# The first loads of a two-layer decoder trunk: a quarter of x in two tiles, two loads of `up` begun by ScalarE, two warm products fewer

## The chip, the cores and the metric

The kernel runs on one core of one Trainium2 chip. The metric is the device time of one execution in microseconds; 0.2% of it is about 2 us. The engines are called by the profile's names: PE (TensorE), with PEld for its weight loads, DVE (VectorE), ACT (ScalarE), POOL (GpSimd) and SP (SyncE). SPq and ACTq are the queues on which SP and ACT issue loads.

## What is computed

Two layers of a decoder trunk on 256 tokens of width 1024. Only the first lines of the first layer matter here:

```python
def rms_norm(x, g):
    xf = x.astype(jnp.float32)
    y = xf * lax.rsqrt(jnp.mean(xf * xf, axis=-1, keepdims=True) + RMS_EPS)
    return (y * g.astype(jnp.float32)).astype(x.dtype)

def swiglu(x, w_gate, w_up, w_down):
    return (jax.nn.silu(x @ w_gate) * (x @ w_up)) @ w_down

for l in range(DEPTH):
    h = h + 0.5 * swiglu(rms_norm(h, ffn1_norm[l]), ffn1_w_gate[l], ffn1_w_up[l], ffn1_w_down[l])
    h = h + hybrid_mixer(...)
    h = h + 0.5 * swiglu(rms_norm(h, ffn2_norm[l]), ffn2_w_gate[l], ffn2_w_up[l], ffn2_w_down[l])
```

The weights of the first feed-forward are 1024 x 2816 for `gate` and `up`, 2816 x 1024 for `down`, in float32.

## The kernel before

Every float32 weight is loaded into a `raw` tile and split into two parts of a shorter type, a high part `wh` (a rounding copy) and a low part `wl` (what is left, by a subtraction). The normalised input is split in the same way into `xhl`. A product is then three products of parts, summed in PSUM: high by high, high by low, low by high. In `ffn` the high weights meet both parts of x in one "wide" product of 512 columns, and the low weights meet the high part in a "narrow" one of 256. The division by the root mean square comes later, so the products can begin before the whole of x is there.

The class `Weights` keeps the loads in order. `issue` (line 78) gives out `raw` tiles, five at a time, and begins their loads with `load` (line 89), on SP's queue; `pump` and `take` run the splits. For the first feed-forward of the first layer the loads are put in order by hand (line 260 on): `by_hand` is 4, so `issue` gives tiles to the first four raws and begins nothing, and the lines behind it call `load` and `load_x` one by one. The first raw of `gate` and of `up` (256 columns, all eight tiles of 128 rows) is cut into three loads: row tiles 0 and 1, row tiles 2 and 3, row tiles 4 to 7. `load_x(mp)` (line 188) loads a quarter of x, 256 of its 1024 columns for all 256 tokens, also on SP's queue. ACT issues one load of its own, the gains of the first norm, and then runs an exponential on a tile of ones, ahead of which its function table is loaded.

So the order on SP's queue is: x 0, gate 0, up 0, x 1, gate 1, up 1, x 2, x 3, gate 2, up 2, and on with the second raws. Each line of this list but gate 2 and up 2 is 256 KB.

What TensorE does meanwhile is written out in `opening` (line 467) and ahead of it. `warm_up(WARM)` runs six products of a tile of ones with itself, whose result nobody reads (float32 operands: each is two passes in the profile). Then the gains are turned into columns (`turn_gains`, line 176), and `turn(0)` transposes the first quarter of x, tile by tile, 128 columns each, two token tiles to each. `warm_up(BRIDGE)` puts three more such products behind it. Then for `m` in 0 and 1: ACT writes the high parts of two tiles of x and VectorE the low parts (`parts`, lines 326 and 329); GpSimd copies the high part of a piece of gate, VectorE makes its low part, ACT copies the high part of a piece of up, GpSimd makes its low part (`split`, lines 477 and 478); TensorE runs gate's wide and narrow products, turns the next quarter of x, and runs up's. At last come the second halves (row tiles 4 to 7), copied by GpSimd (line 533) and ACT (line 117). The engines run their own streams in order, and the streams meet at semaphores.

Of the kernel before, what the change touches and what calls it, by code (L numbers as in the profile page):

```python
# [18 lines left out]
P = 128  # L19
# [15 lines left out]
HID_BUFS = 6  # L35
DOWN_LAG = 4
OUT_TAIL = 3
WARM = 6
BRIDGE = 3
B_TURN, A_ROPE, B_STEP, A_ROOT, A_TURN, SUMS_STEP = 18, 18, 20, 22, 26, 29  # L40


# [13 lines left out]
class Weights:  # L56
# [29 lines left out]
                    self.load(self.n_dma, i)  # L86
            self.n_dma += 1

    def load(self, raw, i):
        at, src = self.raws[raw][1][i]  # L90
        self.nc.sync.dma_start(self.raw_tiles[raw][at], src)  # L91

    def pump(self, count=1, low=None):

# [47 lines left out]
def kernel(ctx: ExitStack, tc: tile.TileContext, x, ffn1_norm, ffn1_w_gate, ffn1_w_up, ffn1_w_down,  # L142
                      mix_norm, w_in, forget_bias, a_q_norm, a_k_norm, b_q_norm, b_k_norm, c_q_norm, c_k_norm,
                      w_out, ffn2_norm, ffn2_w_gate, ffn2_w_up, ffn2_w_down, const, out):
    nc = tc.nc
# [7 lines left out]
    at = ctx.enter_context(tc.tile_pool(name="at", bufs=1))  # L153
# [19 lines left out]
    def load_gains(i, g, eng):  # L173
        eng.dma_start(rows[i], g.rearrange("l (k p) -> (l k) p", p=P))
# [10 lines left out]
    G.affine_select(out=ident, in_=ones, pattern=[[-1, P]], compare_op=ALU.is_equal, fill=0.0, base=0,  # L185
                    channel_multiplier=1)

    def load_x(mp):
        cols = slice(256 * mp, 256 * mp + 256)
        nc.sync.dma_start(trunk[:, :, cols], x[0].rearrange("(t p) d -> p t d", p=P)[:, :, cols])  # L190

    load_x(0)
    load_gains(0, ffn1_norm, nc.scalar)
    A.activation(tmp(P), ones, AF.Exp)

# [8 lines left out]
    W = Weights(tc, raw_pool, split_pool)  # L204
# [57 lines left out]
    W.issue()  # L262
    for m in range(2):
        if m:
            load_x(m)
        for i in range(2):
            W.load(i, m)
    for mp in range(2, 4):
        load_x(mp)
    for i in range(2):  # L270
        W.load(i, 2)
    for m in range(2):
# [107 lines left out]
    def ffn(norm, nxt, aside=None, first=False):  # L380
# [86 lines left out]
        def opening():  # L467
# [20 lines left out]
            def turn(mp):  # L488

                ps = []  # L490
                for m in (2 * mp, 2 * mp + 1):
                    ps.append(bank("acc")[:, :S])
                    for t in range(2):
                        T.transpose(ps[-1][:, t * P:(t + 1) * P], trunk[:, t, m * P:(m + 1) * P], ident)  # L494
                return ps
# [11 lines left out]
            xT = turn(0)  # L507
            warm_up(BRIDGE)
            for m in range(2):
# [673 lines left out]
    def warm_up(n, begin=False):  # L1183
        for i in range(n):
            mm(warm[:, :P], ones, ones, begin and i == 0, i == n - 1)

    warm_up(WARM, True)
    norm = Norm(0, 0)
# [40 lines left out]
```

## Time and profile before

| | us |
|---|---|
| three runs | 1038.13, 1038.09, 1037.77 (median 1038.09) |
| the profiled execution | 1038.33 |
| its span, from the first to the last instruction | 1036.6 |
| PE, busy | 1032.3 |
| DVE, busy | 808.9 |
| ACT, busy | 591.8 |
| POOL, busy | 148.2 |

The span is what the trace covers; 1.7 us of the execution lie around it. Matmuls are pipelined and their ends are modelled, so a PE that is busy throughout may still stand for a tenth of a microsecond here and there; starts are the safer reading. In a timeline a line is: start, length, engine, line of the kernel, operation, what it writes and reads, shape, count, and in brackets the idle time of the engine before it with what ended it. All loads move on the same 16 DMA engines: 181.61 MB in the whole run, at a mean of 175 GB/s.

### The profile page before, as it was taken

The page shows a single profiled execution, that of the slowest core. Times are in us where ns is not written, and L with a number is a line of the kernel's source. Part 1 is how long each engine was busy: PE and PEld are TensorE (multiplying, and loading weights), DVE is VectorE, ACT ScalarE, POOL GpSimd, SP SyncE. Part 2 cuts the span into 40 slices and gives each one's busy share as a digit, 9 for nine tenths or more (in the row PEclk, how much of TensorE's full clock was granted, in tenths as well). Part 3 has the DMA queues.
Part 4 walks back from the last instruction along what each step waited for, and adds up shares of the span by engine and source line. Part 5 has one row for each costly group of instructions (what it writes and reads, how often), then busy time and mean ns, then how long its engine had stood idle before and what let it go on. Part 6 is the DMA issues. An engine that isn't in the chain of part 4 may idle for free.

```text
span 1036.6 us, 15084 instructions
## 1 busy us (share of the span) xinstructions
PE 1032.3 (100%) x5641; PEld 898.8 (87%) x5641; DVE 808.9 (78%) x1537; ACT 591.8 (57%) x1045; POOL 148.2 (14%) x177
## 2 busy tenths in 40 slices
PE   9999999999999999999999999999999999999998
PEld 8888888898888888888888888888988988888887
DVE  6978778789876877777788777787898768777776
ACT  6655555666854655555465555557676546555552
POOL 2003000167800000000000110002766000000000
PEclk9999999999999999999999999999999999999999
DMA  9674656555431364645645564664555224554631
GB/s 320 222 244 157 214 185 198 182 190 174 154 131 42 123 230 144 236 163 206 200 163 195 180 219 150 241 185 174 163 194 172 83 67 159 182 199 167 232 134 40
DMA packets 130808, 181.61 MB, mean 175 GB/s; under 512 B 7040, under 2 KB 104624, under 8 KB 130736
## 3 DMA queue, kind: packets, MB, share of 16 engines
q1 hardware_dynamic: 130704, 180.66, 51.5%
q8 instruction: 44, 0.72, 0.3%
q14 instruction: 28, 0.23, 0.1%
q10 hardware_dynamic: 32, 0.01, 0.0%
HBM read 179.60 MB, written 1.05 MB: 174 GB/s over the span
## 4 chain that ended last, share of the span: by engine, by line
PE 99%; DMA 1%; SPq 0%; DVE 0%; issue 0%
PE ps_gu L302 66%; PE ps_acc L302 30%; PE ps_acc L337 1%; PE ps_gu L1038 1%; PE ps_gu L1137 1%; DMA trunk<-in_x_dram 1%; PE ps_acc L739 0%; PE ps_acc L1038 0%; PE ps_gu L1071 0%; PE ps_acc L494 0%; SPq L91 0%; PE ps_acc L363 0%; PE ps_acc L1071 0%; SPq L190 0%; DVE trunk L376 0%
## 5 line engine op out<-in xcount | busy, mean ns | idle before, releaser
L121 DVE TENSOR_TENSOR wl<-raw,wh 128x1024 fp32r<-128x1024 f32 (+2 forms) x342 | 416.9, 1225 | 24.9 <-ACT wh L117 24.9
L117 ACT CAST wh<-raw 128x1024 fp32r<-128x1024 f32 (+2 forms) x341 | 343.0, 1036 | 5.7 <-PE ps_gu L302 4.9
L302 PE MATMUL ps_gu<-xhl,wh 128*128 128x512 f32 x1408 | 330.4, 390 | 0.0
L302 PEld LDWEIGHTS ps_gu<-xhl,wh 128*128 128x128 f32 x1408 | 262.7, 188 | 53.9 <-ACT wh L117 0.4
L302 PEld LDWEIGHTS ps_gu<-xhl,wl 128*128 128x128 f32 x1408 | 176.1, 191 | 4.2 <-issue 0.2
L302 PE MATMUL ps_gu<-xhl,wl 128*128 128x256 f32 x1408 | 179.1, 283 | 0.0
L302 PE MATMUL ps_gu<-wh,xhl 128*128 128x512 f32 (+2 forms) x512 | 157.2, 377 | 0.0
L441 DVE TENSOR_TENSOR tmp<-ps_gu,tmp 128x256 f32<-128x256 f32 x176 | 72.9, 422 | 107.7 <-ACT tmp L440 107.4
L302 PE MATMUL ps_acc<-wh,hh 128*128 128x512 f32 (+1 forms) x352 | 137.2, 390 | 0.0
L302 PE MATMUL ps_acc<-wl,hh 128*128 128x512 f32 (+1 forms) x352 | 137.0, 389 | 0.0
L302 PE MATMUL ps_acc<-wh,hl 128*128 128x512 f32 (+1 forms) x352 | 136.5, 388 | 0.0
L440 ACT COPY tmp<-ps_gu 128x256 f32<-128x256 f32 x176 | 63.5, 371 | 93.3 <-PE ps_gu L302 93.1
L302 PEld LDWEIGHTS ps_gu<-wh,xhl 128*128 128x128 f32 x512 | 94.8, 188 | 14.6
L455 ACT CAST hh<-tmp 128x256 fp32r<-128x256 f32 x80 | 32.6, 407 | 120.0 <-DVE tmp L452 120.0
L302 PE MATMUL ps_gu<-wl,xhl 128*128 128x512 f32 (+2 forms) x256 | 95.7, 374 | 0.0
L447 ACT ACTIVATE tmp<-tmp 128x256 f32<-128x256 f32 x88 | 36.9, 419 | 81.9 <-DVE tmp L445 81.6
L313 POOL TENSOR_TENSOR y_n<-msq,minus_half 128x2 f32<-128x2 f32 x6 | 6.8, 1141 | 529.7 <-DVE msq L312 529.7
L302 PEld LDWEIGHTS ps_acc<-wh,hl 128*128 128x128 f32 x352 | 66.1, 188 | 13.9
L302 PEld LDWEIGHTS ps_acc<-wh,hh 128*128 128x128 f32 x352 | 66.2, 188 | 12.6
L302 PEld LDWEIGHTS ps_acc<-wl,hh 128*128 128x128 f32 x352 | 66.3, 188 | 12.2
L302 PEld LDWEIGHTS ps_gu<-wl,xhl 128*128 128x128 f32 x256 | 48.2, 188 | 6.7
L326 ACT ACTIVATE xhl<-ps_acc,gT 128x256 fp32r<-128x256 f32 x48 | 19.1, 474 | 39.2 <-PE ps_acc L337 35.7
(221 smaller groups left out, 1010.8 us busy)
## 6 DMA issues: line engine op xcount, KB each, us to landing
raw<-in_ffn_w_down_dram SPq DMA_DIRECT2D x44, 1024.0 KB, 4.9
raw<-in_ffn_w_gate_dram SPq DMA_DIRECT2D x42, 1024.0 KB, 6.6
raw<-in_ffn_w_up_dram SPq DMA_DIRECT2D x42, 1024.0 KB, 7.5
raw<-in_w_in_dram SPq DMA_DIRECT2D x24, 1024.0 KB, 4.9
raw<-in_w_out_dram SPq DMA_DIRECT2D x8, 1024.0 KB, 4.9
raw<-in_w_in_dram SPq DMA_DIRECT2D x4, 768.0 KB, 4.9
raw<-in_w_in_dram SPq DMA_DIRECT2D x4, 656.0 KB, 4.0
raw<-in_ffn_w_gate_dram SPq DMA_DIRECT2D x3, 512.0 KB, 7.1
```

The source lines that it names most:

```text
L117: self.nc.scalar.copy(hv, src)
L121: (engine or self.nc.vector).tensor_tensor(lv, self.srcs[self.n_low], hv.bitcast(F32), op=ALU.subtract)
L302: T.matmul(o, l, r, start=start, stop=stop, skip_group_check=True)
L313: G.tensor_tensor(y, dst, minus_half[:, :n], op=ALU.pow)
L326: A.activation(self.h[:, m], src, AF.Copy, scale=gT[:, self.col + m:self.col + m + 1])
L337: T.transpose(ps[:, i, t * P:(t + 1) * P], trunk[:, t, (2 * mp + i) * P:(2 * mp + i + 1) * P], ident)
L440: A.copy(o, ps[:, 1])
L441: V.tensor_tensor(o, ps[:, 0], o, op=ALU.add)
L447: A.activation(th, t_, AF.Tanh, scale=0.5)
L455: (V.tensor_copy if late else A.copy)(hh, t_)
L1038: T.transpose(b[:, j * P:(j + 1) * P], pj[i][:, j * P:(j + 1) * P], ident)
L1137: T.transpose(b[:66, i * S + t * P:i * S + (t + 1) * P], src[t][:, 2 * hp_ + i, :], ident)
```

## The change

`WARM` goes from 6 to 5 and `BRIDGE` from 3 to 2. `load_x` counts in tiles of 128 columns now; the first quarter of x is begun as two loads of one tile, the other three quarters as one load of two tiles each. `load` takes a queue, and `up`'s first two loads are begun by ACT, behind its exponential in its stream, in place of SP. The order on SP's queue becomes: x tile 0, x tile 1, gate 0, x 1, gate 1, x 2, x 3, gate 2, up 2, and on as before; on ACT's: the gains, up 0, up 1. PE's order is the same but for the two products; those of VectorE and GpSimd are the same.

```diff
-WARM = 6
-BRIDGE = 3
+WARM = 5
+BRIDGE = 2
...
-    def load(self, raw, i):
+    def load(self, raw, i, queue=None):
         at, src = self.raws[raw][1][i]
-        self.nc.sync.dma_start(self.raw_tiles[raw][at], src)
+        (queue or self.nc.sync).dma_start(self.raw_tiles[raw][at], src)
...
-    def load_x(mp):
-        cols = slice(256 * mp, 256 * mp + 256)
+    def load_x(k, n=2):
+        cols = slice(P * k, P * (k + n))
         nc.sync.dma_start(trunk[:, :, cols], x[0].rearrange("(t p) d -> p t d", p=P)[:, :, cols])
 
-    load_x(0)
+    load_x(0, 1)
+    load_x(1, 1)
     load_gains(0, ffn1_norm, nc.scalar)
     A.activation(tmp(P), ones, AF.Exp)
...
     for m in range(2):
         if m:
-            load_x(m)
+            load_x(2)
         for i in range(2):
-            W.load(i, m)
-    for mp in range(2, 4):
-        load_x(mp)
+            W.load(i, m, nc.scalar if i else None)
+    for k in (4, 6):
+        load_x(k)
     for i in range(2):
         W.load(i, 2)
```

## The prediction

> **What bounds the kernel now.** First the page: the busy table, then the chain that ended last.
>
> ```profile
> PE 1032.3 (100%) x5641; PEld 898.8 (87%) x5641; DVE 808.9 (78%) x1537; ACT 591.8 (57%) x1045; POOL 148.2 (14%) x177
> ...
> PE 99%; DMA 1%; SPq 0%; DVE 0%; issue 0%
> PE ps_gu L302 66%; PE ps_acc L302 30%; PE ps_acc L337 1%; PE ps_gu L1038 1%; PE ps_gu L1137 1%; DMA trunk<-in_x_dram 1%; PE ps_acc L739 0%; PE ps_acc L1038 0%; PE ps_gu L1071 0%; PE ps_acc L494 0%; SPq L91 0%; PE ps_acc L363 0%; PE ps_acc L1071 0%; SPq L190 0%; DVE trunk L376 0%
> ```
>
> TensorE makes up 99% of the chain; the one other piece is a load of x. So a microsecond won or lost in the opening reaches the end only if TensorE has no later wait that swallows it. The view of waits for TensorE's weight loads over the whole run tells that (total, times, longest):
>
> ```profile
> PEld ps_gu L302 <- ACT pT L1040: 0.7, 2, 0.4
> PEld ps_gu L302 <- ACT wh L117: 0.4, 1, 0.4
> PEld ps_acc L494 <- DMA trunk<-in_x_dram: 0.3, 1, 0.3
> ```
>
> The last two lie in the opening; the first, in two pieces, belongs to the mixer's heads. Behind the opening there is nearly nothing to hide in: a shift there goes to the end one for one. The opening itself is the next view, the timeline of TensorE (start, length, instruction, count):
>
> ```profile
> 1.04 2.93 PE L302 MATMUL ps_gu<-ones 128*128 128x128 f32 x12 [1.04 <-POOL minus_half L184]
> 3.90 0.28 PE L178 MATMUL ps_gu<-ident,tmp 16*128 16x16 f32 x1
> 4.12 1.11 PE L494 MATMUL ps_acc<-ident,trunk 128*128 128x128 f32 x4
> 5.03 1.31 PE L302 MATMUL ps_gu<-ones 128*128 128x128 f32 x6
> 6.10 1.18 PE L302 MATMUL ps_gu<-xhl,wh 128*128 128x512 f32 x4
> 7.11 0.63 PE L302 MATMUL ps_gu<-xhl,wl 128*128 128x256 f32 x4
> 7.81 0.66 PE L494 MATMUL ps_acc<-ident,trunk 128*128 128x128 f32 x4
> ```
>
> Warm products (two passes each, x12 for six), the gains' transpose, four transposes of x's first quarter, three bridge products, and at 6.10 the first useful products. At 7.81 comes the second quarter of x, the 0.3 us wait above. Also to be seen: the same four transposes last 1.11 us at 4.12 and 0.66 at 7.81, so TensorE is slow until about 6 us.
>
> **The change, part by part.** I follow three gates: the first useful product (6.10), the turn of x's second quarter (7.81), and up's second half (the wait on L117).
>
> *Gate 1, TensorE's own queue.* One warm product less is two passes: (3.90 - 1.04)/12 = 0.24 us each, 0.48 us. The gains' transpose could start at 3.42, x's turn at 3.64. The bridge loses two passes of 1.31/6 = 0.22, 0.44 us. TensorE alone would be at the useful products at 6.10 - 0.92 = 5.2. What it needs there:
>
> ```profile
> trunk<-in_x_dram SPq DMA_DIRECT2D x1, 256.0 KB, 3.0
> raw<-in_ffn_w_gate_dram SPq DMA_DIRECT2D x1, 256.0 KB, 3.3
> tmp<-in_ffn_norm_dram ACTq DMA_DIRECT2D x1, 8.0 KB, 2.6
> ```
>
> These are the first loads, with the time from issue to landing. And where they are issued, on SP's queue and (second fence) on ScalarE:
>
> ```profile
> 0.79 0.43 SPq L190 DMA_DIRECT2D trunk<-in_x_dram  x1
> 1.27 0.46 SPq L91 DMA_DIRECT2D raw<-in_ffn_w_gate_dram  x1
> 1.78 0.46 SPq L91 DMA_DIRECT2D raw<-in_ffn_w_up_dram  x1
> 2.29 0.47 SPq L190 DMA_DIRECT2D trunk<-in_x_dram  x1
> 2.80 0.47 SPq L91 DMA_DIRECT2D raw<-in_ffn_w_gate_dram  x1
> 3.31 0.47 SPq L91 DMA_DIRECT2D raw<-in_ffn_w_up_dram  x1
> ```
>
> ```profile
> 0.78 0.46 ACTq L174 DMA_DIRECT2D tmp<-in_ffn_norm_dram  x1
> 1.27 1.28 ACT L194 ACT_TABLE_LOAD   x1 [1.27 <-PEq L1217]
> 2.56 0.31 ACT L194 ACTIVATE tmp<-ones 128x128 f32<-128x128 f32 x1
> 4.84 0.90 ACT L326 ACTIVATE xhl<-ps_acc,gT 128x256 fp32r<-128x256 f32 x2 [1.97 <-PE ps_acc L494]
> 6.19 0.62 ACT L477 CAST wh<-raw 128x512 fp32r<-128x512 f32 x1 [0.45 <-DMA raw<-in_ffn_w_up_dram]
> ```
>
> Gains land at 0.78 + 2.6 = 3.38, just before 3.42. x's first quarter landed at 0.79 + 3.0 = 3.79, so it would now be late for 3.64 as one load; as two, its first tile has half the bytes ahead. How fast bytes move is the view of windows (last columns: DMA share, GB/s):
>
> ```profile
> 2.00:3.00 1.00, 1.00 (x7) 1.00 (x6) 0.00 (x0) 0.86 (x2) 0.00 (x0) 1.00 0.68 216
> 3.00:4.00 1.00, 1.00 (x6) 0.78 (x5) 0.00 (x0) 0.00 (x0) 0.00 (x0) 1.00 1.01 330
> 4.00:5.00 1.00, 1.00 (x5) 0.96 (x6) 0.17 (x1) 0.16 (x1) 0.39 (x1) 1.00 0.93 288
> 5.00:6.00 1.00, 1.00 (x7) 1.00 (x6) 0.65 (x2) 0.74 (x2) 0.22 (x1) 1.00 0.84 244
> 6.00:7.00 1.00, 1.00 (x7) 0.83 (x7) 0.86 (x2) 0.62 (x1) 0.10 (x1) 1.00 0.74 215
> 7.00:8.00 1.00, 0.94 (x8) 0.72 (x7) 0.00 (x0) 0.00 (x0) 1.00 (x1) 1.00 0.89 277
> 8.00:13.00 5.00, 5.00 (x33) 4.41 (x33) 2.88 (x7) 4.30 (x11) 3.25 (x4) 1.00 1.09 371
> ```
>
> Summed up, 216 KB have moved by 3.0 us, 546 by 4.0, 834 by 5.0, 1078 by 6.0, 1293 by 7.0. 128 KB at 330 GB/s are 0.39 us: tile 0 lands near 3.4, in time. Tile 1 lands near 3.79 if nothing shares the engines and near 4.2 if up's load does byte for byte; it is needed at 3.64 + 1.11/2 = 4.2. No wait, or a tenth.
>
> The operands come next: VectorE's low parts of x and GpSimd's copy of gate.
>
> ```profile
> 5.35 0.91 DVE L329 SCALAR_TENSOR_TENSOR xhl<-ps_acc,gT,xhl 128x256 fp32r<-128x256 f32 x2 [0.95 <-ACT xhl L326]
> ```
>
> ```profile
> 4.61 0.61 POOL L477 CAST wh<-raw 128x512 fp32r<-128x512 f32 x1 [2.89 <-DMA raw<-in_ffn_w_gate_dram]
> ```
>
> The first low part ended at 5.35 + 0.46 = 5.81, with the earlier turn 5.33: the bridge may be shorter, and the cover left is about 0.1 us. Gate is the weak one. It landed at 1.27 + 3.3 = 4.57 (the copy waited for it), 0.67 after its last of 512 KB had moved (3.90). Now it is issued a slot later, at 1.78, with x's 256 KB still ahead on SP's queue, and up's loads beside it. Nothing of up ahead: 4.57, the copy done at 5.22, useful products near 5.4. Up sharing byte for byte since some 110 KB of x had gone (0.5 us later, at 216 GB/s): 512 + 400 KB, moved at 5.3, landed at 5.95, the copy done at 6.6. I take the middle, 6.0: 0.1 us earlier than 6.10 instead of 0.9.
>
> *When does up start?* ScalarE issues both loads behind its table load (1.27) and the exponential, which ends at 2.87. The trace of before has no load issued behind a table load. Bounds: at once, at SP's spacing, 1.3 and 1.8; or after the exponential, 2.9 and 3.4. I take the first: the issues stand on ACTq, apart from the engine, and the nearest row (0.78) has an issue with nothing to wait for. Up itself has time: before, it was copied at 6.19, 0.45 us after ScalarE was free, and used after 7.81.
>
> *Gate 2.* The chain view gives the second quarter of x its time:
>
> ```profile
> 2.29 5.47 DMA trunk<-in_x_dram
> ```
>
> Landed at 7.76; TensorE, done with the products of 7.11, waited. So what gate 1 gains is taken back here unless this load comes earlier. Its last byte was 1024 KB into the order (moved at 5.8, landed 2.0 later, as some engines lag). In the new order SP's queue has 768 KB up to there, issued at the same 2.29, and up's 512 KB on the other queue are all issued before it. None ahead: 768 KB, 4.8, landed 6.75 (-1.0). All ahead: 1280 KB, 6.9, landed 8.9 (+1.15). All ahead, but two queues holding the engines at the 371 GB/s of the last row from 3.0 on: moved at 5.9, landed between 6.5 and 7.9 with either lag. The nearest row is the 7.76 itself; I take 8.0: +0.25.
>
> [...]
>
> *Gate 3.* Up's second half:
>
> ```profile
> 13.36 1.05 ACT L117 CAST wh<-raw 128x1024 fp32r<-128x1024 f32 x1 [0.56 <-DMA raw<-in_ffn_w_up_dram]
> ```
>
> ScalarE waited 0.56 us for that load, TensorE's weights 0.4 for the copy, its products less; I take 0.2. The bytes up to this load are the same 3 MB, so it lands as before, unless the slow stretch fills: 3 to 8 us moved 1354 KB where 371 GB/s give 1855, at most 1.35 us earlier. If TensorE comes 0.25 later, its wait of 0.2 is gone, and +0.05 is left.
>
> *The rest.* SP issues one load less, so the second halves of gate and up are issued 0.5 us earlier, behind loads that still wait: nothing. VectorE's and GpSimd's orders stay. x's shorter rows are a shape that before doesn't show: between nothing and one more such load (0.39 us), I take the tenth at tile 1.
>
> **Sum.** Queue -0.9, taken back by operands (to -0.1) and by the load at gate 2 (to +0.25), less the wait at gate 3: about +0.1 us. The profiled execution took 1038.33 us (span 1036.6 and 1.7 around it), so 1038.4; the median of three runs lies 0.24 lower, 1038.09, so I forecast 1038.2.
>
> **Rivals.**
> 1. *Two queues fill the slow stretch.* For it: the DMA share is 0.74 to 0.93 from 4 to 7 us with loads waiting on one queue. Against: they may lag for reasons that a second queue doesn't touch. Then gates 2 and 3 both come early and TensorE gets at most 0.7 (5.4 for 6.1) + 0.26 + 0.2 = 1.15; likely 0.7: 1037.4.
> 2. *Up crowds out gate and x*, with no better flow: +1.15 at gate 2, less 0.2 to 0.4 at gate 3: +0.8, 1038.9. For it: up's loads now stand ahead of what is needed first.
> 3. *Slower, the clock.* The 1.11 against 0.66 show that full speed came some 5 us after the first product at 1.04, while TensorE hardly stood still (0.2 us before 3.90). With two products less it may stand from 5.2 to 6.0, and at tile 1. If such a hole counts as a new start at 4.2, full speed comes at 9.3: 3.2 us of work at 1.7 to 2 times its time cost 2.2 to 3.2, less 0.46 of waits that vanish: +1.7 to +2.7, say +2.2, 1040.3. It decides once the hole passes what the clock forgives; the 0.2 us were forgiven. [...]
> 4. *Up isn't begun early*: ScalarE holds it behind the exponential (2.9). Then gate is undisturbed, and gate 2 sees at most the old 1024 KB: -0.2, 1037.9.
>
> **How the numbers follow.** Forecast (-0.3 to +0.4) 0.42; rival 1 0.30; rival 2 0.18; rival 3 0.06; rival 4 0.04. The range takes in rival 1 to its end (-1.15) and rival 2 (+0.95) with a little of rival 3: 1037.0 to 1039.3. About 0.2%, 2.08 us, is what a measurement of this kernel can tell from no change. Nothing here gives that much gain (0.01); only rival 3 loses it (0.05); within, 0.94.
>
> **What would show it.** In the new timeline: the gains' transpose at 3.4 and x's turn at 3.6 (gate 1's queue); ACTq's issues of up at 1.3 and 1.8 (or 2.9); the copy of gate on GpSimd at 5.3 rather than 4.6, and the first useful products near 6.0; the second quarter's transposes at 8.0; the wait on L117 small or gone. Useful products whose four take well over 1.18 us would show rival 3; GB/s near 371 between 4 and 8 us rival 1. I am wrong if the second quarter turns before 7.5 or after 8.5.

## The result, and the profile after

The changed kernel took 1040.64 us (median of 11 runs, 1039.19 to 1041.89), the kernel before 1037.96 (11 runs, 1037.74 to 1038.32): 2.7 us more, ratio 1.0024, 95% interval 1.0016 to 1.0032. The forecast was 1038.2 with a range to 1039.3, so the time lies outside it, on the slower side. The profiled execution took 1041.61 us, the second longest of the eleven, its span 1039.9. The ratios, here and below, follow the means of the runs, not their medians; two runs of the experiments that were disturbed, one of 1131.3 and one of 1276.25 us, are not in them. Lines behind the added call of `load_x` stand one higher than before (L302 is L303, L478 is L479).

TensorE's timeline of the changed kernel is the view to start with (start, length, instruction, count, idle time ahead):

```profile
1.04 2.50 PE L303 MATMUL ps_gu<-ones 128*128 128x128 f32 x10 [1.04 <-POOL minus_half L184]
3.48 0.28 PE L178 MATMUL ps_gu<-ident,tmp 16*128 16x16 f32 x1
3.69 0.69 PE L495 MATMUL ps_acc<-ident,trunk 128*128 128x128 f32 x2
4.93 0.69 PE L495 MATMUL ps_acc<-ident,trunk 128*128 128x128 f32 x2 [0.56 <-DMA trunk<-in_x_dram]
5.42 1.06 PE L303 MATMUL ps_gu<-ones 128*128 128x128 f32 x4
7.25 2.07 PE L303 MATMUL ps_gu<-xhl,wh 128*128 128x512 f32 x4 [0.77 <-POOL wh L478]
9.12 1.14 PE L303 MATMUL ps_gu<-xhl,wl 128*128 128x256 f32 x4
10.06 1.05 PE L495 MATMUL ps_acc<-ident,trunk 128*128 128x128 f32 x4
10.77 2.06 PE L303 MATMUL ps_gu<-xhl,wh 128*128 128x512 f32 x4
12.62 0.86 PE L303 MATMUL ps_gu<-xhl,wl 128*128 128x256 f32 x4
13.33 1.08 PE L303 MATMUL ps_gu<-xhl,wh 128*128 128x512 f32 x4
```

Three things differ from the opening before. TensorE stands still twice: 0.56 us between the two tiles of x, 0.77 us ahead of the first useful products, which come at 7.25 instead of 6.10. The four wide products then last 2.07 us where they lasted 1.18, the narrow ones 1.14 instead of 0.63, and so on until 13.3 us. And the second quarter of x is turned at 10.06 instead of 7.81, with no load named as its releaser. TensorE's products, matched one by one, begin 1.2 us later than before at the first useful one and 3.6 us later at 13.2 us. Until about 30 us 0.5 us of that comes back, and from there on the two executions stand a constant 3.1 us apart: all of the loss is made in the opening.

The waits of TensorE's weight loads between 4 and 13 us (total, times, longest) name what it stood for:

```profile
PEld ps_gu L303 <- POOL wh L478: 1.1, 1, 1.1
PEld ps_acc L495 <- DMA trunk<-in_x_dram: 1.0, 1, 1.0
PEld ps_gu L303 <- DVE wl L479: 0.4, 1, 0.4
```

GpSimd's and VectorE's timelines tell why the first and the third are there. Those of the kernel before first, GpSimd's row and VectorE's:

```profile
6.89 1.28 POOL L478 TENSOR_TENSOR wl<-raw,wh 128x512 fp32r<-128x512 f32 x1 [1.68 <-ACT wh L477]
```

```profile
6.18 0.68 DVE L478 TENSOR_TENSOR wl<-raw,wh 128x512 fp32r<-128x512 f32 x1
```

Then those of the changed kernel, in the same order:

```profile
6.59 0.61 POOL L478 CAST wh<-raw 128x512 fp32r<-128x512 f32 x1 [4.87 <-DMA raw<-in_ffn_w_gate_dram]
7.17 1.27 POOL L479 TENSOR_TENSOR wl<-raw,wh 128x512 fp32r<-128x512 f32 x1
```

```profile
7.23 1.76 DVE L479 TENSOR_TENSOR wl<-raw,wh 128x512 fp32r<-128x512 f32 x1 [0.58 <-POOL wh L478]
```

GpSimd waited for gate's first load until 6.59; before, its copy began at 4.61. ScalarE's copy of up no longer comes behind gate's low part, but ahead of gate's copy, so both subtractions become ready together: GpSimd's starts at 7.17, VectorE's 0.06 later, and VectorE's lasts 1.76 us instead of 0.68. It ends at 8.99, that is 0.55 after GpSimd's (8.44).

Last, ScalarE's own rows, and the windows from 3 to 8 us (last column GB/s), which were 330, 288, 244, 215 and 277 before:

```profile
1.27 1.28 ACT L195 ACT_TABLE_LOAD   x1 [1.27 <-PEq L1218]
1.34 0.97 ACTq L91 DMA_DIRECT2D raw<-in_ffn_w_up_dram  x2
```

```profile
3.00:4.00 1.00, 1.00 (x6) 0.71 (x5) 0.17 (x1) 0.00 (x0) 0.00 (x0) 1.00 0.83 237
4.00:5.00 1.00, 0.45 (x3) 0.07 (x2) 0.08 (x1) 0.47 (x1) 0.00 (x0) 1.00 1.09 361
5.00:6.00 1.00, 1.00 (x5) 1.00 (x6) 0.41 (x1) 0.34 (x1) 0.00 (x0) 1.00 1.04 337
6.00:7.00 1.00, 0.48 (x3) 0.18 (x1) 0.48 (x1) 0.64 (x2) 0.41 (x1) 1.00 0.95 292
7.00:8.00 1.00, 0.75 (x2) 0.65 (x3) 0.77 (x1) 0.00 (x0) 1.00 (x2) 1.00 0.96 320
```

Up's loads were issued at 1.34, during the table load, and the engines moved 1310 KB from 4 to 8 us instead of 1024 (the four windows added up), though less than before in the microsecond ahead. The bytes came faster, and TensorE lost time all the same. How much of the difference is the second queue's doing these two runs don't tell: in the traces of the experiments the same four windows add up to 1045 to 1230 KB with all these loads on SP's queue, and to 1265 to 1347 KB with up's on ACT's.

### The profile page after: what moved, and what is told of

Read it like the earlier page. It is cut to its first block, busy times and chain, and to the rows that moved or that the text cites. A ratio compares the mean times of both kernels' runs of the same rounds, so it can differ in the third digit from the quotient of the medians.

```text
span 1039.9 us, 15077 instructions
## 1 busy us (share of the span) xinstructions
PE 1034.2 (99%) x5637; PEld 900.2 (87%) x5637; DVE 810.0 (78%) x1537; ACT 591.6 (57%) x1045; POOL 149.4 (14%) x177
## 4 chain that ended last, share of the span: by engine, by line
PE 99%; issue 0%; POOL 0%; DVE 0%; POOLq 0%
PE ps_gu L303 66%; PE ps_acc L303 30%; PE ps_acc L338 1%; PE ps_gu L1039 1%; PE ps_gu L1138 1%; PE ps_acc L740 0%; PE ps_acc L1039 0%; PE ps_gu L1072 0%; PE ps_acc L495 0%; PE ps_acc L364 0%; PE ps_acc L1072 0%; POOL wh L478 0%; DVE trunk L377 0%; POOL ident L185 0%; PE ps_gu L178 0%
## 5 line engine op out<-in xcount | busy, mean ns | idle before, releaser
L117 ACT CAST wh<-raw 128x1024 fp32r<-128x1024 f32 (+2 forms) x341 | 343.1, 1036 | 4.9 <-PE ps_gu L303 4.9
L303 PE MATMUL ps_gu<-xhl,wh 128*128 128x512 f32 x1408 | 331.8, 391 | 0.8 <-POOL wh L478 0.8
L303 PEld LDWEIGHTS ps_gu<-xhl,wh 128*128 128x128 f32 x1408 | 263.8, 189 | 54.8 <-POOL wh L478 1.1
L303 PEld LDWEIGHTS ps_gu<-xhl,wl 128*128 128x128 f32 x1408 | 176.8, 192 | 4.4 <-DVE wl L479 0.4
L303 PE MATMUL ps_gu<-xhl,wl 128*128 128x256 f32 x1408 | 179.7, 284 | 0.0
L303 PE MATMUL ps_gu<-wh,xhl 128*128 128x512 f32 (+2 forms) x512 | 157.2, 377 | 0.0
L303 PE MATMUL ps_acc<-wh,hh 128*128 128x512 f32 (+1 forms) x352 | 137.2, 390 | 0.0
L303 PE MATMUL ps_acc<-wl,hh 128*128 128x512 f32 (+1 forms) x352 | 137.0, 389 | 0.0
L303 PE MATMUL ps_acc<-wh,hl 128*128 128x512 f32 (+1 forms) x352 | 136.5, 388 | 0.0
L303 PEld LDWEIGHTS ps_gu<-wh,xhl 128*128 128x128 f32 x512 | 94.8, 188 | 14.6
L303 PE MATMUL ps_gu<-wl,xhl 128*128 128x512 f32 (+2 forms) x256 | 95.7, 374 | 0.0
L303 PEld LDWEIGHTS ps_acc<-wh,hl 128*128 128x128 f32 x352 | 66.1, 188 | 13.8
L303 PEld LDWEIGHTS ps_acc<-wh,hh 128*128 128x128 f32 x352 | 66.2, 188 | 12.6
L303 PEld LDWEIGHTS ps_acc<-wl,hh 128*128 128x128 f32 x352 | 66.3, 188 | 12.2
L303 PEld LDWEIGHTS ps_gu<-wl,xhl 128*128 128x128 f32 x256 | 48.2, 188 | 6.6
```

The lines of the kernel that those rows point to most:

```text
L117: self.nc.scalar.copy(hv, src)
L303: T.matmul(o, l, r, start=start, stop=stop, skip_group_check=True)
```

## The experiments

Two theories stood at first. **C**: the two holes keep TensorE's clock low, and that is the loss. **L**: gate and x's second tile land later, and that is the loss. A third, **D**, was formed after the first eight runs: VectorE's and GpSimd's subtractions get in each other's way. Each kernel ran 11 times beside the kernel before (the last one 9 times), and is compared with the runs of that kernel in its own group. The medians of before were 1037.86 for the first four kernels, 1037.73 for the next four, 1038.01 for the three after, 1037.88 for the last.

**The parts alone: products, loads, queue.** Starting from the changed kernel, its loads without its products:

```diff
-WARM = 5
-BRIDGE = 2
+WARM = 6
+BRIDGE = 3
```

> The loads of the changed kernel (x's first quarter as two tiles, up's first two loads on ACT), with the old six warm and three bridge products. Theory C (clock): the loads leave TensorE standing before the first useful products, and with fewer products the holes are long enough to keep its clock low (full speed at 13.1 us instead of 6.0). More products shorten the holes; full speed comes back to 6 to 7 us and only the later start of the useful products (7.2 for 6.1) is left: +0.5 to +1.2 us, 1038.5 to 1039.2. Theory L (loads): the late gate load is the whole of it and the products are beside the point: as the changed kernel, +2.7, 1040.6.

Measured: 1039.37 us, +1.5 (ratio 1.0018, 1.0009 to 1.0026), between the two expectations. In its trace the four wide products last 1.19 us again, behind a hole of only 0.32 us, and TensorE waits 0.62 us for VectorE's low part of gate. The reverse, the kernel before with WARM 5 and BRIDGE 2:

> The old loads, with five warm and two bridge products. Theory C: a hole of 0.2 to 0.5 us before the first useful products, with everything else on time; if that is enough to keep the clock low, +1.5 to +2.5 (1039.5 to 1040.5), with a spread of over a microsecond between runs; if it is forgiven, -0.3 to 0. Theory L: nothing is late, so 0 to -0.3 us.

Measured: 1037.59, -0.3 (0.9998, 0.9989 to 1.0007). Less warming alone does no harm, and perhaps some good: the useful products came at 5.55, behind a hole of only 0.18 us. Then the changed kernel with up's loads back on SP's queue:

```diff
-            W.load(i, m, nc.scalar if i else None)
+            W.load(i, m)
```

> The changed kernel with up's first two loads back on SP's queue, in their old places; x in two tiles and the fewer products stay. Theory L, with the crowding put down to ACT's queue: gate lands near 4.7 instead of 6.5, useful products at 5.6, the time 0 to -0.5 us from before. Theory C: as the run with the products alone: 0 to -0.3 if the hole is forgiven, +1.5 to +2.5 if not.

Measured: 1038.49, +0.6 (1.0009, 1.0000 to 1.0018). GpSimd's copy of gate begins at 5.01 here, not at 6.59, and there is no hole between the tiles of x: the second tile had landed whole at 3.58 us, in the changed kernel at 4.89. And the kernel before with up's first two loads on ACT's queue and nothing else:

> The old kernel with only up's first two loads moved to ACT's queue. Theory L: gate lands 1 to 2 us later, useful products near 7, +0.7 to +2.7 us. Theory C: three bridge products run out near 6.1 and a hole of about 1 us follows; if the clock isn't at full speed by then, +1.5 to +2.5, else +0.5 to +1.0.

Measured: 1037.92, +0.1 (1.0003, 0.9994 to 1.0012). The copy of gate begins at 5.47 instead of 4.61, but the three bridge products last until it is done, and the first useful product comes at 6.14. So neither the products nor the queue does the harm alone; the loads as a whole do more than half of it.

**x in two tiles.** The kernel before with the split quarter alone, and the changed kernel without it. The edit of the second, on the changed kernel, is this:

```diff
-    load_x(0, 1)
-    load_x(1, 1)
+    load_x(0)
```

The first:

> The kernel before with only x's first quarter split into two tiles. Gate's load moves back by one issue on SP's queue (0.5 us). Theory L: gate lands 0.1 to 0.5 us later, useful products between 6.1 and 6.4, 0 to +0.3 us. Theory C: the bridge covers it, the clock is at full speed near 6: 0 to +0.3.

Measured: 1038.68, +0.95 (1.0011, 1.0002 to 1.0020). Gate is issued one slot later here, and GpSimd's copy of it begins at 5.49 instead of 4.61. Not all of the loss is in the trace: the profiled execution took 1039.37 us and its span 1037.0, so 2.4 us lie around the span instead of 1.7. What that is stays open. The second:

> The changed kernel with x's first quarter as one load again: up's loads on ACT and the fewer products stay. Theory L: gate is issued an issue earlier and lands at 5.5 to 6, useful products near 6.7: +0.5 to +1.5. Theory C: TensorE still stands before them, so the clock stays low: +1.5 to +2.7, with a spread of over a microsecond.

Measured: 1038.34, +0.6 (1.0007, 0.9998 to 1.0016). Gate is held back less (its copy begins at 5.65), and there is no hole between the tiles.

Both parts of the loads hold gate back, then, as the starts of its copy show: 4.61, 4.62 and 4.82 in the three traces with the old loads, 5.01 and 5.49 with x in two tiles alone, 5.47 and 5.65 with up on ACT's queue alone. With both it is 5.75, 6.03, 6.14, 6.50 and 6.59 in five traces with the same loads, so a single trace is good for half a microsecond at most, and that of the change is the latest of the five. One line from each of three kernels, x in two tiles, up on ACT's queue, and both (the loads alone):

```profile
5.49 0.61 POOL L478 CAST wh<-raw 128x512 fp32r<-128x512 f32 x1 [3.77 <-DMA raw<-in_ffn_w_gate_dram]
5.47 0.61 POOL L477 CAST wh<-raw 128x512 fp32r<-128x512 f32 x1 [3.75 <-DMA raw<-in_ffn_w_gate_dram]
5.75 0.61 POOL L478 CAST wh<-raw 128x512 fp32r<-128x512 f32 x1 [4.03 <-DMA raw<-in_ffn_w_gate_dram]
```

**The clock.** The holes are filled with products on the tile of ones: two between the tiles of x, three more on the bridge.

```diff
-BRIDGE = 2
+BRIDGE = 5
...
                 for m in (2 * mp, 2 * mp + 1):
+                    if m == 1:
+                        warm_up(2)
```

> The changed kernel with its loads, and products that nobody reads put into TensorE's two holes: two between the transposes of x's first and second tile, and five instead of two in the bridge. Theory C (clock): TensorE stands nowhere before its useful products, full speed comes near 6 us, and only the later start (7.2 to 7.5 for 6.1) is left: +0.7 to +1.4 us, 1038.7 to 1039.4, and a spread between runs as small as before's. Theory L (loads): the useful products start as late as in the changed kernel and it takes as long, +2.7, 1040.6.

Measured: 1039.43, +1.7 (1.0017, 1.0008 to 1.0026). TensorE's timeline:

```profile
5.63 1.28 PE L303 MATMUL ps_gu<-ones 128*128 128x128 f32 x10
7.16 1.21 PE L303 MATMUL ps_gu<-xhl,wh 128*128 128x512 f32 x4 [0.24 <-POOL wh L478]
8.97 0.74 PE L303 MATMUL ps_gu<-xhl,wl 128*128 128x256 f32 x4 [0.60 <-DVE wl L479]
9.55 0.60 PE L497 MATMUL ps_acc<-ident,trunk 128*128 128x128 f32 x4
```

The first useful products come no earlier than after (7.16 for 7.25), so nothing was gained in the loads; but the four last 1.21 us again. The other side: the kernel before with a hole made in it, by leaving out the bridge.

```diff
             xT = turn(0)
-            warm_up(BRIDGE)
```

> The kernel before, with all its loads, without the three bridge products: TensorE stands from 5.0 to about 5.9. Theory C: the clock stays low past 6 us, +1.5 to +2.5 us and a spread of over a microsecond between runs. Theory L: no load is touched, the useful products start at 5.9: 0 to -0.2 us.

Measured: 1038.89, +1.2 (1.0007, 0.9998 to 1.0016), less than theory C had, and in two groups: four runs from 1037.44 to 1037.64, seven from 1038.03 to 1039.52. The interval, over both groups, takes in no change; but six of the eleven lie above the slowest of the 33 runs of before (1038.27). The profiled run (1039.52) is of the second:

```profile
4.11 1.11 PE L494 MATMUL ps_acc<-ident,trunk 128*128 128x128 f32 x4
5.98 2.04 PE L302 MATMUL ps_gu<-xhl,wh 128*128 128x512 f32 x4 [0.75 <-DVE xhl L329]
7.82 1.05 PE L302 MATMUL ps_gu<-xhl,wl 128*128 128x256 f32 x4
8.67 1.05 PE L494 MATMUL ps_acc<-ident,trunk 128*128 128x128 f32 x4
```

Here the loads are those of before and the first useful products are even 0.12 us earlier, yet four of them last 2.04 us. One hole of 0.75 us at about 5.2 us is enough for that; by the first group's times it doesn't come to it in every run. A hole behind the point of full speed did no such thing: in the changed kernel without x's tiles (+0.6) TensorE stood for 0.98 us, and four of its products lasted 1.19 us:

```profile
6.32 1.19 PE L302 MATMUL ps_gu<-xhl,wh 128*128 128x512 f32 x4 [0.98 <-POOL wh L477]
```

That is one of the quick runs of this kernel (1037.78). Four of its eleven lie between 1039.00 and 1039.86, and no trace tells where full speed came in those.

The records of the granted clock in the traces agree: they begin at 6.0 us before, at 13.1 after, at 10.6 with the hole made, at 5.6 with the holes filled, and at 4.9 in this last kernel, ahead of its hole. How far apart the two speeds lie is in the starts: in the changed kernel the transposes begin 0.213 us apart from 10.27 to 10.70, and 0.108 from 14.24 to 14.57, a factor of 1.97. (The clock column of the windows reads 1.00 ahead of these starts too: it counts time without a record as full.)

The same records tell what a hole did. In the 14 traces of this case, those of the experiments further down included, full speed lasts 1027.41, 1030.83 or 1034.24 us: three lengths, 3.41 us apart. Count back from where it begins, in steps of 3.41 us. In the last step TensorE never stood for more than 0.28 us; in every step before it, it stood for at least 0.56 us, or its products had yet to begin. In the changed kernel the steps are 2.88 to 6.30 us, with the hole of 0.56, 6.30 to 9.71, with that of 0.77, and 9.71 to 13.12, with none. So full speed came at the end of the first step without a long hole. Where the steps lie differs from run to run: in the ten traces with no hole ahead of it, full speed began anywhere from 4.85 to 6.93 us, though TensorE's first product always came at 1.04.

**The two subtractions.** With the holes filled 1.7 us were still lost, and TensorE waited 0.60 us for VectorE. The kernel with the holes filled, and up's first low part on VectorE, behind gate's:

```diff
-                split(1, m, A.copy, G)
+                split(1, m, A.copy, G if m else V)
```

> Against the kernel with the holes filled (1039.43): up's first low part is taken on VectorE, behind the gate's, instead of on GpSimd beside it. Theory D (two subtractions beside each other on VectorE and GpSimd slow one another, 0.68 to 1.77 us, and TensorE waits 0.60 for it): the gate's low part takes 0.68 again, the wait of TensorE on it goes, 1038.8 (1038.5 to 1039.1). Rival L (what is lost is the gate's late landing alone): the gate's low part still takes over 1.5 us, or the wait goes and the time stays at 1039.4 (1039.2 to 1039.7).

Measured: 1038.51, +0.5 (1.0004, 0.9995 to 1.0013; all runs within 0.6 us). VectorE's and TensorE's timelines:

```profile
6.67 1.29 DVE L479 TENSOR_TENSOR wl<-raw,wh 128x512 fp32r<-128x512 f32 x2 [0.27 <-POOL wh L478]
```

```profile
6.69 1.19 PE L303 MATMUL ps_gu<-xhl,wh 128*128 128x512 f32 x4 [0.20 <-POOL wh L478]
7.72 0.64 PE L303 MATMUL ps_gu<-xhl,wl 128*128 128x256 f32 x4
8.20 0.60 PE L497 MATMUL ps_acc<-ident,trunk 128*128 128x128 f32 x4
```

Both subtractions one after the other take 1.29 us on VectorE, less than the one took beside GpSimd's. From the first useful product to the turn of x it is 1.51 us, with the holes filled alone it was 2.39: 0.9 us, as theory D said. That gate came earlier in this profiled run (6.03 for 6.50) is not its doing. That the order decides which of the two takes longer is to be seen in the changed kernel without x's tiles. There VectorE was first, and GpSimd's took 1.63 us instead of 1.28; first VectorE's row, then GpSimd's:

```profile
6.29 0.69 DVE L478 TENSOR_TENSOR wl<-raw,wh 128x512 fp32r<-128x512 f32 x1 [0.47 <-POOL wh L477]
```

```profile
6.50 1.63 POOL L478 TENSOR_TENSOR wl<-raw,wh 128x512 fp32r<-128x512 f32 x1 [0.24 <-ACT wh L477]
```

So in the changed kernel 0.06 us decided about 1.1 us of VectorE's time (1.76 for 0.68). What holds the later one up no trace names. It didn't quite stand until the other was done: VectorE's ended at 8.99, 0.13 us sooner than GpSimd's end and its own 0.68 us make (8.44 + 0.68), and GpSimd's in the last rows at 8.13, again 0.13 sooner (6.98 + 1.28).

**Gate ahead of x's second tile**, in the kernel with the holes filled:

```diff
     load_x(0, 1)
-    load_x(1, 1)
...
             W.load(i, m, nc.scalar if i else None)
+            if i == m == 0:
+                load_x(1, 1)
```

> Against the kernel with the holes filled (1039.43): gate's first load is issued ahead of x's second k tile, so 0.5 us earlier. Theory L (the gate's landing sets the first useful product): first useful product 0.4 earlier, near 6.7, 1039.0 (1038.7 to 1039.3). Rival X (x's second k tile, now issued 0.5 later, becomes the last to land): first useful product no earlier than 7.1, 1039.5 (1039.3 to 1040). Theory D says that either way the gate's low part takes 1.8 us beside up's.

Measured: 1040.56, +2.6 (1.0021, 1.0012 to 1.0030). Gate came earlier (GpSimd's copy at 5.66), but x's second tile became the last:

```profile
6.33 0.44 PE L498 MATMUL ps_acc<-ident,trunk 128*128 128x128 f32 x2 [1.13 <-DMA trunk<-in_x_dram]
```

Rival X was right in kind and, by the median, too cheap by a microsecond. In this execution (1039.14) full speed came at 5.0 us, ahead of the hole; seven of the eleven runs lie above 1040.3, which a hole ahead of full speed would explain, but none of them has a trace. With both edits:

> Both of the edits above in the kernel with the holes filled: gate's first load ahead of x's second k tile, up's first low part on VectorE. If the late gate and the two subtractions beside each other are together what the loads cost (theories L and D), 1038.3 (1038.0 to 1038.8), within 0.6 of the kernel before. If only one of them holds, 1038.8 to 1039.2; if neither, 1039.4.

Measured: 1040.87, +2.9 (1.0025, 1.0016 to 1.0034): none of the expected values. The hole at x's second tile was 0.59 us here, and the products behind it were slow. The bridge of ten passes took 2.34 us, the one with the holes filled 1.28, and held up the useful products to 8.29:

```profile
5.82 0.69 PE L498 MATMUL ps_acc<-ident,trunk 128*128 128x128 f32 x2 [0.59 <-DMA trunk<-in_x_dram]
6.30 2.34 PE L304 MATMUL ps_gu<-ones 128*128 128x128 f32 x10
8.29 1.64 PE L304 MATMUL ps_gu<-xhl,wh 128*128 128x512 f32 x4
```

So whether an early gate would bring the last half microsecond back these two don't tell: the edit opened a new hole.

**The low part on VectorE alone**, in the changed kernel, with its holes left (the diff is the one line shown above):

> The changed kernel with up's first low part on VectorE instead of GpSimd and nothing else: the two holes in TensorE's queue stay. In its profile TensorE waited 0.4 us for the gate's low part, against 0.6 with the holes filled, since its four products ahead of that took 2.07 us. If the prices add whatever the clock (theory D alone, additive): 0.9 off, 1039.7 (1039.4 to 1040.0). If the late clock covers the slow subtraction (theory C sets the time while TensorE is at half speed): at most the 0.4 that is waited, 1040.4 (1040.1 to 1040.7), spread over more than 2 us, full speed after 9 us in the profile.

Measured: 1040.39, +2.5 (1.0024, 1.0014 to 1.0034). TensorE:

```profile
6.80 2.07 PE L303 MATMUL ps_gu<-xhl,wh 128*128 128x512 f32 x4 [0.28 <-POOL wh L478]
8.67 1.06 PE L303 MATMUL ps_gu<-xhl,wl 128*128 128x256 f32 x4
9.53 0.78 PE L495 MATMUL ps_acc<-ident,trunk 128*128 128x128 f32 x4
```

The wait for VectorE is gone and the time stays, as theory C said. With this the four cases stand side by side, each against the kernel before:

| | low part on GpSimd | low part on VectorE |
|---|---|---|
| holes as they are | +2.7 (the change) | +2.5 |
| holes filled | +1.7 | +0.5 |

Filling the holes is worth 2.0 us where nothing else holds TensorE up, and 1.0 where VectorE does; moving the low part is worth 1.2 us with the clock up, and 0.2 with it low. The two prices overlap, since slow products hide a slow subtraction: in the changed kernel the narrow products follow the wide ones without idle time, with the holes filled TensorE stood for 0.60 us ahead of them. The right column's two intervals (1.0014 to 1.0034 and 0.9995 to 1.0013) don't meet, so the clock's price is shown; the step from +1.7 to +0.5 has intervals that overlap at 1.0008 to 1.0013, and rests on the rows as well.

Of the versions tried, only less warming alone lies below the kernel before, by 0.3 us, and its interval takes in no change.

## Why the prediction was wrong

- *What bounds the kernel* held nearly: of a shift of 3.6 us in the opening, 3.1 reached the end in the two profiled runs.
- *Gate 1, TensorE's queue* held in its starts: the gains' transpose came at 3.48, x's turn at 3.69 (said: 3.4 and 3.6). Its 0.92 us were a little too much, 0.73 in the run with the products alone (6.10 before; there 5.55, less the 0.18 that it stood): the bridge's passes were priced by their length, 0.22 us, while their starts lie (6.10 - 5.03)/6 = 0.18 apart. At the end that run was 0.3 us shorter, within its interval of no change.
- *Gate 1, the operands* is the step that failed first. "Useful products near 6.0" became 7.25, and the end of the range for gate, landed at 5.95, was passed: its last piece landed at 6.53, and GpSimd's copy waited for it until 6.59. The rate was not what failed: from 2 to 5 us 824 KB moved, and 834 before. The order was. The sum let up's loads and gate's go byte for byte; in the trace up's first load had landed whole at 5.08, before the first piece of gate (5.18), and 15 of the 16 DMA engines had brought theirs of up's second load by 6.42. x's second tile, "no wait, or a tenth", cost a hole of 0.56 us. The sums of bytes leave out that TensorE waits for the last piece of a load: 15 engines had brought theirs of x's second tile by 4.11 us, the last one at 4.89. Gate issued 0.5 us later, with up beside it, was copied 2.0 us later here, and 1.1 to 2.0 us later in the five traces with these loads.
- *Gate 2*: 8.0 was forecast, 10.06 came, and the sign "after 8.5" had been named for being wrong. But the load was not the reason: it had landed at 7.43, before at 7.76, and no row has TensorE waiting for it. TensorE came late to it, by gate 1 and by its clock. Whether up's second queue moved more bytes or only began them earlier the runs don't settle: from 4 to 8 us the nine traces with up on ACT's queue moved 1265 to 1347 KB and the five without 1024 to 1230, but up was issued earlier in the nine as well.
- *Gate 3* held: the wait on L117 is gone from the view. Up's second half was not issued 0.5 us earlier, as *The rest* had it, but at 6.55 instead of 5.36; it landed at 12.55, before at 13.34, all the same.
- *Up at once, or behind the exponential*: at once (1.34 us, during the table load). Rival 4 is out.
- *Rival 1* came true in its sign and not in its time: 361 and 337 GB/s in the first two windows, for a kernel 2.7 us slower. A better flow was spent on up, which had time, and gate came late for it. The slow stretch that it was to fill was in part that one run's: with the same loads, two other traces moved 1181 and 1183 KB from 4 to 8 us, not 1024. *Rival 2* was right in the mechanism and named the wrong victim: up crowds out gate, not x's second quarter.
- *Rival 3* got a chance of 0.06 and 1040.3 us; the kernel took 1040.64, with the sign that had been named, four useful products in well over 1.18 us (2.07). Its holes are the ones it named, ahead of the first useful product and at tile 1, and its price of 2.2 us is near the 2.0 that the right column of the table shows. That its time comes so near is in part luck: full speed was to come at 9.3, a fixed time behind the hole, and came at 13.1, behind two steps with a hole each, and part of the loss is the subtractions', which it did not have. The 2 of its "1.7 to 2 times" has no row beside it in the prediction; the starts of the transposes before, 0.213 us apart from 4.39 to 4.81 and 0.109 from 7.97 to 8.19, make it 1.95. What failed is the chance, and this is the costliest failure: the two times that this rival starts from (1.11 against 0.66 us) showed how slow TensorE was until about 6 us, the forecast itself opened a hole from 5.2 to 6.0, ahead of that point, and "the 0.2 us were forgiven" was taken for more than it says.
- *Missing altogether*: the two subtractions. "VectorE's and GpSimd's orders stay" was true, and the moment at which they meet did not stay. Before, ScalarE's copy of up ended with gate's low part, at 6.8 to 6.9 us, so that GpSimd's began 0.03 us behind VectorE's end, by the old order of loads and nothing else. The price is 0.9 to 1.2 us once the clock is up.

What is left of the loss with the holes filled and the low part on VectorE, +0.5 us, goes with gate's landing by the rows (first useful product 6.69 for 6.10), and is not settled: within the interval of that run it may be nothing.

## What to carry to other kernels

This opening was a race of a few loads whose order mattered more than their flow (1310 KB for 1024 from 4 to 8 us, and 2.7 us more): begin first what is waited for first, even if engines stand half empty, and count each slot of delay by the landing of the whole load. Warm products don't only fill time; while TensorE isn't yet at full speed, a hole shorter than a microsecond behind them can cost more than its own length (with a hole of 0.75 us the span of the profiled run was 1.2 us longer, though the useful products began earlier), so take them away only where the operand behind them surely comes earlier. And where a change moves the moment at which an engine's work becomes ready, look at what it then runs beside: here VectorE's and GpSimd's subtractions held each other up (1.76 us for 0.68 on the one, 1.63 for 1.28 on the other).

## What the runs showed of the hardware

- A hole of 0.75 us ahead of full speed moved the start of the clock's record from 6.0 to 10.6 us (hole made), two of 0.56 and 0.77 to 13.1 (after); 0.98 us behind full speed cost nothing in the products' time (1.19 us for four, 1.18 before). With the hole made, runs fall into two groups, their middles about 1.6 us apart. In the 14 traces the lengths of full speed lie 3.41 us apart (1027.41, 1030.83, 1034.24), and it began from 4.85 to 6.93 us where no hole came ahead of it. That the two groups come from this spread, as a hole falls ahead of full speed in some runs and behind it in others, is the author's estimate and not shown, since each kernel has one trace.
- VectorE's 128x512 subtraction takes 0.68 us alone and 1.76 when GpSimd's began 0.06 us ahead; GpSimd's takes 1.28 alone and 1.63 when VectorE's began 0.21 ahead.
- Loads that stand behind a table load on ScalarE are issued during it: at 1.34 us, with the table load from 1.27 to 2.55.
- A load of 128 KB of x begun as the second on its queue, with up's loads on ACT's, let TensorE wait until 4.93 us, and begun as the third, behind gate's, until 6.33 or 5.82: 0.5 us later in the queue, 0.9 to 1.4 later on TensorE. With all loads on SP's queue it had landed by 3.6 us (3.52 and 3.58 in two traces).
